# One more pair of row tiles by Strassen's scheme in the output product of a two-layer encoder, and earlier token sums

## The chip, the cores and the metric

The kernel runs on one core of one Trainium2 chip. Its time is device microseconds (us), the median of repeated runs. The core has a TensorE (in the profile PE for matmuls and PEld for weight loads), a VectorE (DVE), a ScalarE (ACT), a GpSimd (POOL), and queues that issue DMAs; nearly all DMAs here are issued by SyncE (SP).

## What is computed

Two layers, each on x of 256 tokens by 2048 columns in float32:

```python
for l in range(DEPTH):                       # DEPTH = 2
    h = rmsnorm(x, norm_g[l])
    proj = h @ w_in[l]                       # 2048 x 7168, split into ten groups
    y_a = conv3(a_c * a_x) * a_b * silu(a_g)     # 768 columns: 6 row tiles of y
    y_d = differential attention, 6 heads        # 768 columns: 6 row tiles
    y_m = attention into 256 memory tokens, 4 heads  # 512 columns: 4 row tiles
    y = concatenate([y_a, y_d, y_m]) @ w_out[l]  # 2048 x 2048
    x = x + y
```

The change lies in the last product, y @ w_out[l], and in how its operands are prepared.

## The kernel before

**Products.** Every float32 operand is split into a high and a low part in float32r (`hi`, a cast on ACT, and `lo`, the difference on DVE), and one product of a 128x128 token tile with a 128x512 weight tile is three matmuls: high by high, high by low, low by high (`products`, L305; `product`, L351). The activations are kept transposed, 16 row tiles k of 128 columns each, with 256 tokens: `yT` holds y. Tiles 0 to 5 are the conv group, 6 to 11 the differential heads, 12 to 15 the memory heads. Tile 6 + n is ready once head n is done; `made` records it.

**Pieces.** `block` goes through row tiles two at a time. One such weight piece is 256 rows by 512 columns of a weight matrix, 512 KB. `load_w` issues its DMA on SP into one of four `raw` buffers (L291), casts it on ACT (L294) and makes the low part on DVE (L295), into one of four `hi` and four `lo` buffers. A piece then feeds 12 matmuls: two row tiles, two token halves, three matmuls each. A `hi` or `lo` buffer is free again when the matmuls of the piece four before are done. After each piece `run_side` advances the tasks: generators that do the work beside the products (attention, gates, turns through DRAM) a few instructions at a time; `later(g, n)` makes a task due n pieces on.

**Order.** What is wrapped in `pin` (`keep_in_program_order`) keeps the program's order on its engine; the rest is placed by a list scheduler that works on a timeline at build time. DMAs of `carry` (turns through DRAM) and the wide loads below are pinned.

**The output product before.** PSUM has four accumulator banks (`acc`) and four more (two `s`, two `t`), which attention uses earlier. w_out's 2048 columns are four blocks b of 512. Blocks 0 and 1 are begun with the ten head tiles (five pieces each), then finished with the six conv tiles (three pieces each), because the conv group comes last. `leave` adds a finished block to the residual `xs` (L1230) and, in layer 0, starts the turn of that quarter for the next layer. Blocks 2 and 3 are then made together: some pairs of row tiles (two pairs in layer 0, three in layer 1, `places`) go by Strassen's scheme in Winograd's form over both column blocks (`seven`), the rest by `block`, block 2 first.

**`seven`.** For one pair of row tiles and 1024 columns it loads two 128x1024 weight tiles (`wide`, L373, 512 KB each), makes seven weight operands from them with four subtractions (L380), a half-size split `one` and three full splits (L377), and does seven products of three matmuls (L351) where the plain way has eight. Products land in the two accumulators of the near block, the two of the far block, and four banks x1, x5, x6, x7 in `s` and `t`. `collect` later adds those four to the residual: a copy on ACT (L1266) and eight additions on DVE (L1262). The token side needs four sums per pair, made by `token_sums` (L356 to L366) in the task `all_sums`: one `f` addition, four additions of 128 columns, a cast and a difference. They live in buffers that earlier work leaves free (`mkT0`, `mkT1`, `v`). The task is started after the C_C block, eight pieces before the output product begins.

In this text T0, T1 and so on are the weight pieces counted from the start of a layer's output product. With the heads of block 0 at T0 to T4 and of block 1 at T5 to T9, the conv pieces follow at T10 to T15.

Of the kernel before, what the change touches and what calls it, by code (L numbers as in the profile page):

```python
# [10 lines left out]
F32 = mybir.dt.float32  # L11
# [7 lines left out]
P = 128  # L19
# [13 lines left out]
NB = 512  # L33
# [15 lines left out]
def encoder(ctx: ExitStack, tc: tile.TileContext, x, mem, norm_g, w_in, conv_w, conv_b,  # L49
# [21 lines left out]
    def nm(s):  # L71
        uid[0] += 1
        return f"{s}_{uid[0]}"
# [140 lines left out]
    def later(g, n):  # L214
        due[id(g)] = chunk[0] + n
        return g
# [151 lines left out]
    def seven(stat, k, sums, w, col0, c_near, c_far, x, first, last, homes, meanwhile):  # L368


        a, b = (pl.tile([P, 2, NB], F32, tag=tag, name=nm("wide")) for pl, tag in homes)
        for j, raw in enumerate((a, b)):
            pin(nc.sync.dma_start(raw.rearrange("p j c -> p (j c)"), w[(k + j) * P:(k + j + 1) * P, col0:col0 + 2 * NB]))  # L373

        def split(src, to=None):
            hi, lo = to or parts_tiles()
            return ((hi, pin(nc.scalar.copy(hi, src))), (lo, pin(nc.vector.tensor_tensor(lo, src, hi.bitcast(F32), ALU.subtract))))  # L377

        def minus(dst, v, u):
            pin(nc.vector.tensor_tensor(dst, v, u, ALU.subtract))  # L380

        def side_of(parts, j):
            return [v[:, j] for v, _ in parts]

        one = keep.tile([P, 2, 1, NB], F32R, tag="mga", name=nm("one"))
        b11 = split(a[:, 0:1], (one[:, 0], one[:, 1]))
        minus(a[:, 0], a[:, 1], a[:, 0])
        minus(a[:, 1], b[:, 1], a[:, 1])
        b2 = split(b)
        minus(b[:, 1], b[:, 1], a[:, 0])  # L390
        minus(b[:, 0], b[:, 0], b[:, 1])
        meanwhile()
        t13 = split(a)
        t42 = split(b)

        def tokens(j, t):
            return [stat[:, part, k + j, t * P:(t + 1) * P] for part in range(2)]

        def summed(i):
            return [sums[:, part, i] for part in range(2)]  # L400

        x1, x5, x6, x7 = x
        product(tokens(0, 0), x1, side_of(b11, 0), first, last)
        product(tokens(1, 0), c_near[0], side_of(b2, 0), False, False)
        product(summed(3), c_far[0], side_of(b2, 1), first, False)
        product(summed(0), x5, side_of(t13, 0), first, last)
        product(summed(2), x7, side_of(t13, 1), first, last)
        product(tokens(1, 1), c_near[1], side_of(t42, 0), False, False)
        product(summed(1), x6, side_of(t42, 1), first, last)
# [54 lines left out]
    def sheet(home, tag, n=NB // P):  # L464
        return home.tile([P, NA, n, NT, B], F32, tag=tag, name=nm("sh"))
# [200 lines left out]
    def mem_scores(l, h, st):  # L666
        while l not in queries:
            yield 1
        qT, parts = queries[l]
        q, k, g = qT[:, h], mkT[l][:, h], mgain[:, l:l + 1]  # L670
        qh, ql, kh, kl = (parts[:, j] for j in (2 * (h % 2), 2 * (h % 2) + 1, 4, 5))
        pin(nc.scalar.copy(qh, q))
        pin(nc.vector.tensor_tensor(ql, q, qh.bitcast(F32), ALU.subtract))
        pin(nc.scalar.activation(kh, k, AF.Copy, scale=g))
        pin(nc.vector.scalar_tensor_tensor(kl, k, g, kh.bitcast(F32), ALU.mult, ALU.subtract))
        yield 1
        sc = P ** -0.5
        s = ps_s.tile([P, NT, SEQ], F32, tag="s", name=nm("s"))
        for i in range(NT):
            at = slice(i * P, (i + 1) * P)  # L680
            nc.tensor.matmul(s[:, i, :], qh[:, at], kh, start=True, stop=False)  # L681
            nc.tensor.matmul(s[:, i, :], qh[:, at], kl, start=False, stop=False)  # L682
            nc.tensor.matmul(s[:, i, :], ql[:, at], kh, start=False, stop=True)  # L683
        mx = small.tile([P, NT], F32, tag="mmx", name=nm("mmx"))
        nc.vector.tensor_reduce(mx, s, AX.X, ALU.max)
        nc.vector.tensor_scalar(mx, mx, -sc, None, ALU.mult)
        sm = small.tile([P, NT], F32, tag="msm", name=nm("msm"))
        e = tmp.tile([P, NT, SEQ], F32, tag="e", name=nm("me"))
        for i in range(NT):
            nc.scalar.activation(e[:, i], s[:, i], AF.Exp, bias=mx[:, i:i + 1], scale=sc, accum_out=sm[:, i:i + 1])  # L690
        r = small.tile([P, NT], F32, tag="mr", name=nm("mr"), bufs=6)
        nc.vector.reciprocal(r, sm)
        nc.vector.tensor_tensor(r, r, st[:, HR], ALU.mult)
        for i in range(NT):
            nc.vector.tensor_scalar(e[:, i], e[:, i], r[:, i:i + 1], None, ALU.mult)
        return e

    spare, yTs, gates, summed_heads = {}, {}, {}, set()

    def mem_pair(l, n, st):  # L700
        heads = (2 * n, 2 * n + 1)
# [361 lines left out]
    for l in range(DEPTH):  # L1063
# [9 lines left out]
        def x_block(cols, order=ALLK, **how):  # L1073
            return block(xT, w_in[l], cols, order, rows=x_row_tiles, **how)
# [101 lines left out]
        def both_rows(dst, j0, j1):  # L1176
            return [by_columns(dst[:, :, j0:j1, t]) for t in range(NT)]

        def scaled(dst, acc, by):
            for t in range(NT):  # L1180
                nc.scalar.activation(dst[t], columns(acc[t]), AF.Copy, scale=col(st, by, t))
# [10 lines left out]
        acc = x_block([(C_G, NB)])  # L1192
        gate(0, NB, acc)
        tasks.append(later(turn_bg(list(range(CG))), 9))
        acc = x_block([(C_X, NB)])
        ux = sheet(keep, "bgx", CG)
        scaled(both_rows(ux, 0, 4), acc, R2)
        acc = x_block([(C_C, NB)])
        times(both_rows(ux, 0, 4), acc)
        tasks.append(later(conv([0, 1, 2, 3], ux), 6))  # L1200
        sums = []

        def all_sums(l, yT, sums):
            for n, tag in enumerate(("mkT0", "v") if l + 1 < DEPTH else ("mkT0", "mkT1", "v")):
                while tag == "v" and (l, MH // 2 - 1) not in summed_heads:
                    yield 1
                sums.append(keep.tile([P, 2, 4, P], F32R, tag=tag, name=nm("sums")))
                yield from token_sums(yT, CG + 2 * n, sums[n])
                yield 1

        tasks.append(later(all_sums(l, yT, sums), 1))
        acc = x_block([(C_X + NB, 256), (C_C + NB, 256)])
        scaled(both_rows(ux, 4, 6), [a[:, 0:256] for a in acc], R2)
        times(both_rows(ux, 4, 6), [a[:, 256:512] for a in acc])
# [4 lines left out]
            xT = T_tile("xT")  # L1219
        heads, convs = list(range(CG, KT)), list(range(CG))  # L1220

        accs = [block(yT, w_out[l], [(b * NB, NB)], heads, more=True) for b in range(2)]
        final = l + 1 == DEPTH

        def finish(b, acc, keep_order=lambda i: i):
            for t in range(NT):
# [12 lines left out]
        def leave(b, acc, keep_order=lambda i: i, n=5):  # L1239
            finish(b, acc, keep_order)  # L1240
            if not final:
                tasks.append(later(x_next(xT, l + 1, b), n))

        for b in range(2):
            block(yT, w_out[l], [(b * NB, NB)], convs, acc=accs[b])
            if b == 0:
                leave(b, accs[b])
# [3 lines left out]
        homes = [((tmp, tag),) * 2 for tag in ("sh", "e", "sh")] if final else [((tmp, "sh"),) * 2, ((keep, "bgx"), (keep, "ga"))]  # L1251
        rest = [k for k in heads + convs if not CG <= k < CG + 2 * len(places)]
        near, far = accumulators(), accumulators()
        x = [pl.tile([P, NB], F32, tag=tag, name=nm("x")) for pl, tag in ((ps_s, "s"), (ps_s, "s"), (ps_t, "t"), (ps_t, "t"))]

        def collect(near):

            def at(t, b):
                return xs[:, t, b * NB:(b + 1) * NB]

            def plus(dst, v, u):
                pin(nc.vector.tensor_tensor(dst, v, u, ALU.add))  # L1262

            x1, x5, x6, x7 = x
            u, v = (tmp.tile([P, NB], F32, tag="nat", name=nm("u"), bufs=3) for _ in range(2))
            pin(nc.scalar.copy(u, x1))  # L1266
            plus(at(0, 2), u, at(0, 2))
            plus(u, u, x6)
            plus(v, u, x7)
            yield 1  # L1270
            plus(at(1, 2), v, at(1, 2))
            if not final:
                leave(2, near, n=3)
            plus(u, u, x5)
            plus(at(0, 3), u, at(0, 3))
            yield 1
            plus(v, v, x5)
            plus(at(1, 3), v, at(1, 3))
            if final:
                leave(2, near)  # L1280

        def pair_at(n):
            def run(near):
                seven(yT, paired[n], sums[n], w_out[l], 2 * NB, near, far, x, n == 0, n == len(paired) - 1,
                      homes[n], (lambda: leave(1, accs[1], pin, 4)) if n == 0 else lambda: None)
                if n == len(paired) - 1:
                    tasks.append(later(collect(near), 5))
                run_side(1)
            return run

# [35 lines left out]
```

## Time and profile before

| | us |
|---|---|
| median of 3 runs | 919.62 (919.55 to 919.75) |
| the profiled execution | 919.16 |
| its span in the trace | 917.4 |
| PE busy | 911.9 |
| DVE busy | 720.1 |
| ACT busy | 515.8 |

The span reaches from the first to the last instruction that the profiler recorded; 1.76 us of the profiled execution lie around it. In a line of the timeline the columns are the start, the duration, the engine, the source line, the operation, the tiles (output, then inputs), the shape and the count; a bracket names how long the engine had been idle and who ended it. A duration reaches to the end of the write, so that successive instructions of an engine overlap in it. A line of the stretches table gives, for each engine, busy time and number of instructions, then the granted TensorE clock, the DMA engines' busy share and GB/s. A line of the groups table gives count, busy time and mean duration in ns, then the idle time before.

### The profile page before, as it was taken

What the parts mean: (1) busy time and instruction counts of PE and PEld (TensorE: products, weight loads), DVE (VectorE), ACT (ScalarE), POOL (GpSimd) and SP (SyncE); (2) the same over time, 40 slices, a digit from 0 to 9 for tenths busy, and PEclk for the clock granted to TensorE, in tenths of its full rate; (3) what the DMA queues carried; (4) which work ended last, traced back from release to release, by engine and by line L of the source; (5) the groups of instructions that cost most, each with busy time, mean ns of one, the idle gap of its engine ahead of it and who ended that gap; (6) DMA issues with size and microseconds to landing.
All of it is one profiled execution on the core that took longest, in us unless ns stands there. A gap on an engine that the chain in (4) does not pass through costs nothing.

```text
span 917.4 us, 12407 instructions
## 1 busy us (share of the span) xinstructions
PE 911.9 (99%) x4161; PEld 757.3 (83%) x4161; DVE 720.1 (78%) x1293; ACT 515.8 (56%) x798; POOL 38.3 (4%) x68
## 2 busy tenths in 40 slices
PE   9999999999999999999999999999999999999998
PEld 6888888888888888888888888888888888888887
DVE  5579978857799697677789857878898787588786
ACT  5667645675555556445556544578555565546352
POOL 2435010000000000000000000000000000000000
PEclk9999999999999999999999999999999999999999
DMA  8899878886679998979777867986889998968842
GB/s 288 289 243 248 287 247 229 244 222 197 188 206 238 247 256 235 263 243 241 264 215 228 275 203 213 268 239 178 236 231 221 266 260 227 268 215 234 275 161 92
DMA packets 244560, 215.15 MB, mean 235 GB/s; under 512 B 131976, under 2 KB 171720, under 8 KB 244496
## 3 DMA queue, kind: packets, MB, share of 16 engines
q1 hardware_dynamic: 239520, 208.71, 79.3%
q0 software_dynamic: 3776, 4.59, 2.1%
q10 hardware_dynamic: 1200, 1.07, 0.3%
q8 instruction: 32, 0.52, 0.2%
q14 instruction: 32, 0.26, 0.1%
HBM read 193.30 MB, written 21.00 MB: 234 GB/s over the span
## 4 chain that ended last, share of the span: by engine, by line
PE 99%; DMA 0%; ACT 0%; SPq 0%; DVE 0%; issue 0%; ACTq 0%
PE acc L305 92%; PE x L351 2%; PE po L519 1%; PE acc L351 1%; PE s L627 1%; PE po L749 1%; PE s L626 1%; PE acc L933 1%; PE pt L763 0%; DMA raw<-in_w_mem_kv_dram 0%; PE s L683 0%; PE s L681 0%; PE s L682 0%; PE rest L305 0%; ACT hi L915 0%; SPq L833 0%
## 5 line engine op out<-in xcount | busy, mean ns | idle before, releaser
L305 PE MATMUL acc<-hi,xT 128*128 128x512 f32 x1792 | 558.4, 390 | 0.0
L294 ACT CAST hi<-raw 128x1024 fp32r<-128x1024 f32 x270 | 283.9, 1053 | 277.3 <-PE acc L305 200.0
L295 DVE TENSOR_TENSOR lo<-raw,hi 128x1024 fp32r<-128x1024 f32 x270 | 329.0, 1222 | 126.7 <-ACT hi L294 124.5
L305 PEld LDWEIGHTS acc<-hi,xT 128*128 128x128 f32 x1792 | 336.3, 188 | 69.0
L305 PE MATMUL acc<-lo,xT 128*128 128x512 f32 x896 | 349.2, 390 | 0.0
L305 PEld LDWEIGHTS acc<-lo,xT 128*128 128x128 f32 x896 | 168.2, 188 | 33.6
L305 PE MATMUL acc<-hi,yT 128*128 128x512 f32 (+1 forms) x432 | 134.1, 388 | 0.0
L305 PEld LDWEIGHTS acc<-hi,yT 128*128 128x128 f32 x432 | 81.0, 188 | 16.7
L305 PE MATMUL acc<-lo,yT 128*128 128x512 f32 x216 | 83.7, 388 | 0.0
L305 PE MATMUL acc<-hi,memT 128*128 128x512 f32 x248 | 78.0, 392 | 0.0
L305 PEld LDWEIGHTS acc<-hi,memT 128*128 128x128 f32 x248 | 46.2, 188 | 9.3
L916 DVE SCALAR_TENSOR_TENSOR lo<-raw,cva,hi 128x1024 fp32r<-128x1024 f32 (+1 forms) x34 | 41.0, 1218 | 15.4 <-ACT hi L915 15.1
L305 PE MATMUL acc<-lo,memT 128*128 128x512 f32 x124 | 48.0, 391 | 0.0
L305 PEld LDWEIGHTS acc<-lo,yT 128*128 128x128 f32 x216 | 40.6, 188 | 8.4
L915 ACT ACTIVATE hi<-raw,cva 128x1024 fp32r<-128x1024 f32 (+1 forms) x34 | 36.5, 1101 | 12.4 <-DMA raw<-in_w_mem_kv_dram 12.2
L305 PEld LDWEIGHTS acc<-lo,memT 128*128 128x128 f32 x124 | 23.3, 188 | 5.5 <-DVE lo L916 0.8
L377 ACT CAST hi<-wide 128x1024 fp32r<-128x1024 f32 x15 | 15.6, 1050 | 16.3 <-DVE wide L380 6.9
L637 ACT ACTIVATE e<-e,mx 128x256 f32<-128x256 f32 x48 | 23.8, 500 | 1.4 <-DVE mx L633 1.3
L780 POOL DMA_DIRECT2D xt<-in_x_dram x32 | 21.5, 678 | 19.7 <-DVE rsy L189 13.6
L377 DVE TENSOR_TENSOR lo<-wide,hi 128x1024 fp32r<-128x1024 f32 x15 | 18.1, 1220 | 3.5 <-ACT hi L377 3.3
L264 ACT ACTIVATE xT<-xf,gx 128x256 fp32r<-128x256 f32 x32 | 14.3, 503 | 5.7 <-DVE xf L786 5.0
L631 DVE SCALAR_TENSOR_TENSOR e<-dist,s 128x512 f32<-128x512 f32 x24 | 15.7, 680 | 2.2 <-PE s L627 1.7
(210 smaller groups left out, 765.8 us busy)
## 6 DMA issues: line engine op xcount, KB each, us to landing
raw<-in_w_in_dram SPq DMA_DIRECT2D x192, 512.0 KB, 4.6
raw<-in_w_out_dram SPq DMA_DIRECT2D x54, 512.0 KB, 4.8
raw<-in_w_in_dram SPq DMA_DIRECT2D x64, 256.0 KB, 4.3
raw<-in_w_mem_kv_dram SPq DMA_DIRECT2D x30, 512.0 KB, 6.4
d<-sh SPq DMA_DIRECT2D x88, 128.0 KB, 4.2
sh<-d SPq DMA_DIRECT2D x72, 128.0 KB, 4.1
wide<-in_w_out_dram SPq DMA_DIRECT2D x10, 512.0 KB, 7.0
xs<-in_x_dram SPq DMA_DIRECT2D x4, 512.0 KB, 6.3
```

Of the source, the lines that this page charges most:

```text
L264: both = (nc.scalar.activation(hi, src, AF.Copy, scale=gain), nc.vector.scalar_tensor_tensor(lo, src, gain, hi.bitcast(F32), ALU.mult, ALU ...
L294: nc.scalar.copy(hi, raw)
L295: nc.vector.tensor_tensor(lo_, raw, hi.bitcast(F32), ALU.subtract)
L305: i = nc.tensor.matmul(acc, left, right, start=start, stop=stop)
L351: nc.tensor.matmul(acc, left[a], right[b], start=first and i == 0, stop=last and i == 2)
L377: return ((hi, pin(nc.scalar.copy(hi, src))), (lo, pin(nc.vector.tensor_tensor(lo, src, hi.bitcast(F32), ALU.subtract))))
L519: nc.tensor.matmul(po[:, t, :], eT[:, i, t, k, :], v[:, k, h * P:(h + 1) * P], start=k == 0, stop=k == NT - 1)
L631: nc.vector.scalar_tensor_tensor(e[:, c], dist, -slopes[h], s[c], ALU.mult, ALU.add)
L637: nc.scalar.activation(e[:, c, i], e[:, c, i], AF.Exp, bias=mx[:, c, i:i + 1], accum_out=sm[:, c, i:i + 1])
L780: tc.keep_in_program_order(nc.gpsimd.dma_start(st[:, n], src[n * B:(n + 1) * B].rearrange("p (b r) -> b p r", b=NA)))
L915: both = (nc.scalar.activation(hi[:, j], raw[:, j], AF.Copy, scale=g), nc.vector.scalar_tensor_tensor(lo[:, j], raw[:, j], g, hi[:, j].bit ...
L916: nc.vector.scalar_tensor_tensor(lo[:, j], raw[:, j], g, hi[:, j].bitcast(F32), ALU.mult, ALU.subtract))
```

## The change

In both layers the pair of row tiles 6 and 7 (differential heads 0 and 1) goes through `seven` for the column blocks 0 and 1, too. Blocks 0 and 1 then take four head pieces each (tiles 8 to 15) in place of five, and the wide pair is put between the third and the fourth piece of block 0. Its seven products go to the two accumulators of block 0, the two of block 1 (both pairs of accumulators are now taken up front), and the banks `s` and `t`; `collect`, due four pieces later, adds the four banks to the residual. The wide tiles and the `one` operand use the temporary buffers `sh`, `sh` and `e`. `sums[0]` serves both wide pairs of tiles 6 and 7. The task `all_sums` is started after the C_G block, 16 pieces sooner; it now waits until the two heads' tiles are made, and, for the buffer of the layer's own memory keys, until all memory heads are scored. With the new count the pieces of the output product are T0, T1, T2, the wide pair, the last head piece of block 0 (here p3), four of block 1 (b0 to b3), then the conv pieces V0 to V5. The two-way shape of blocks 2 and 3 stays.

```diff
     def seven(stat, k, sums, w, col0, c_near, c_far, x, first, last, homes, meanwhile):
-        a, b = (pl.tile([P, 2, NB], F32, tag=tag, name=nm("wide")) for pl, tag in homes)
+        a, b = (pl.tile([P, 2, NB], F32, tag=tag, name=nm("wide")) for pl, tag in homes[:2])
...
-        one = keep.tile([P, 2, 1, NB], F32R, tag="mga", name=nm("one"))
+        one = homes[2][0].tile([P, 2, 1, NB], F32R, tag=homes[2][1], name=nm("one"))
...
+        mem_scored.add((l, h))
...
         acc = x_block([(C_G, NB)])
         gate(0, NB, acc)
         tasks.append(later(turn_bg(list(range(CG))), 9))
+        sums = []
+
+        def all_sums(l, yT, sums):
+            for n, tag in enumerate(("mkT0", "v") if l + 1 < DEPTH else ("mkT0", "mkT1", "v")):
+                while not all((id(yT), CG + 2 * n + i) in made for i in range(2)):
+                    yield 1
+                while tag == f"mkT{l}" and not all((l, h) in mem_scored for h in range(MH)):
+                    yield 1
+                while tag == "v" and (l, MH // 2 - 1) not in summed_heads:
+                    yield 1
+                sums.append(keep.tile([P, 2, 4, P], F32R, tag=tag, name=nm("sums")))
+                yield from token_sums(yT, CG + 2 * n, sums[n])
+                yield 1
+
+        tasks.append(later(all_sums(l, yT, sums), 1))
         acc = x_block([(C_X, NB)])
...
         tasks.append(later(conv([0, 1, 2, 3], ux), 6))
-        sums = []
-
-        def all_sums(l, yT, sums):
...
-        tasks.append(later(all_sums(l, yT, sums), 1))
...
-        accs = [block(yT, w_out[l], [(b * NB, NB)], heads, more=True) for b in range(2)]
         final = l + 1 == DEPTH
+        accs = [accumulators() for _ in range(2)]
...
+        def banks():
+            return [pl.tile([P, NB], F32, tag=tag, name=nm("x")) for pl, tag in ((ps_s, "s"), (ps_s, "s"), (ps_t, "t"), (ps_t, "t"))]
+
+        def collect(b, x, then=lambda: None):
...
+            x1, x5, x6, x7 = x
+            u, v = (tmp.tile([P, NB], F32, tag="nat", name=nm("u"), bufs=3) for _ in range(2))
+            pin(nc.scalar.copy(u, x1))
+            plus(at(0, b), u, at(0, b))
+            plus(u, u, x6)
+            plus(v, u, x7)
+            yield 1
+            plus(at(1, b), v, at(1, b))
+            if not final:
+                then()
+            plus(u, u, x5)
+            plus(at(0, b + 1), u, at(0, b + 1))
+            yield 1
+            plus(v, v, x5)
+            plus(at(1, b + 1), v, at(1, b + 1))
+            if final:
+                then()
+
+        x = banks()
+
+        def early_pair(near):
+            seven(yT, CG, sums[0], w_out[l], 0, near, accs[1], x, True, True,
+                  ((tmp, "sh"), (tmp, "sh"), (tmp, "e")), lambda: None)
+            tasks.append(later(collect(0, x), 4))
+            run_side(1)
+
+        for b in range(2):
+            block(yT, w_out[l], [(b * NB, NB)], heads[2:], more=True, acc=accs[b], opened=(b == 1, False),
+                  between={6: early_pair} if b == 0 else {})
         for b in range(2):
             block(yT, w_out[l], [(b * NB, NB)], convs, acc=accs[b])
...
-        x = [pl.tile([P, NB], F32, tag=tag, name=nm("x")) for pl, tag in ((ps_s, "s"), (ps_s, "s"), (ps_t, "t"), (ps_t, "t"))]
+        x = banks()
...
-                      homes[n], (lambda: leave(1, accs[1], pin, 4)) if n == 0 else lambda: None)
+                      (*homes[n], (keep, "mga")), (lambda: leave(1, accs[1], pin, 4)) if n == 0 else lambda: None)
                 if n == len(paired) - 1:
-                    tasks.append(later(collect(near), 5))
+                    tasks.append(later(collect(2, x, lambda: leave(2, near) if final else leave(2, near, n=3)), 5))
```

More of the change, by code (lines that the diff above doesn't have):

```diff
@@ L696, in mem_scores @@
         return e
-    spare, yTs, gates, summed_heads = {}, {}, {}, set()
+    spare, yTs, gates, summed_heads, mem_scored = {}, {}, {}, set(), set()
     def mem_pair(l, n, st):
@@ L1200, in encoder @@
         tasks.append(later(conv([0, 1, 2, 3], ux), 6))
-        sums = []
-        def all_sums(l, yT, sums):
[L1204 to L1209, printed above, removed]
-        tasks.append(later(all_sums(l, yT, sums), 1))
         acc = x_block([(C_X + NB, 256), (C_C + NB, 256)])
@@ L1242, in leave, with at, plus @@
                 tasks.append(later(x_next(xT, l + 1, b), n))
+        def banks():
+            return [pl.tile([P, NB], F32, tag=tag, name=nm("x")) for pl, tag in ((ps_s, "s"), (ps_s, "s"), (ps_t, "t"), (ps_t, "t"))]
+        def collect(b, x, then=lambda: None):
+            def at(t, b):
+                return xs[:, t, b * NB:(b + 1) * NB]
+            def plus(dst, v, u):
+                pin(nc.vector.tensor_tensor(dst, v, u, ALU.add))
+            x1, x5, x6, x7 = x
[24 more added lines that the diff above has]
+                  between={6: early_pair} if b == 0 else {})
         for b in range(2):
@@ L1253, in encoder @@
         near, far = accumulators(), accumulators()
-        x = [pl.tile([P, NB], F32, tag=tag, name=nm("x")) for pl, tag in ((ps_s, "s"), (ps_s, "s"), (ps_t, "t"), (ps_t, "t"))]
[L1256 to L1280, printed above, removed]
+        x = banks()
         def pair_at(n):
```

## The prediction

> **What bounds the kernel now.** First the page: busy time, granted clock and the chain that ended last.
>
> ```profile
> span 917.4 us, 12407 instructions
> ...
> PE 911.9 (99%) x4161; PEld 757.3 (83%) x4161; DVE 720.1 (78%) x1293; ACT 515.8 (56%) x798; POOL 38.3 (4%) x68
> ...
> PEclk9999999999999999999999999999999999999999
> ...
> PE 99%; DMA 0%; ACT 0%; SPq 0%; DVE 0%; issue 0%; ACTq 0%
> ```
>
> PE is busy for all but 5.5 us, the chain is PE alone, and the clock is full in every slice. A busy PE need not be a full one, so next comes the view of waits, for PE:
>
> ```profile
> PE warm L128 <- DVE zeros L123: 1.2, 1, 1.2
> PE acc L933 <- ACT hi L915: 0.8, 1, 0.8
> ```
>
> These are all its waits, 2.0 us, and both lines belong to the start (warm-up and the first memory matmuls). Nowhere in the output products does PE wait. What a matmul then costs is the step from one start to the next, not its 0.39 us. The timeline of PE, first and last of 13 successive starts in a Strassen pair and the piece behind it:
>
> ```profile
> 469.76 0.39 PE L351 MATMUL x<-lo,sums 128*128 128x512 f32 x1
> ...
> 472.48 0.39 PE L305 MATMUL acc<-lo,yT 128*128 128x512 f32 x1
> ```
>
> Twelve steps in 2.72 us: 0.2267 us for one, and 2.72 us for a weight piece of 12. So the kernel is a row of matmuls without holes. It can gain only by fewer of them, and loses as soon as a weight piece is split too late.
>
> How late is too late is the lead: the time from the end of a piece's split on DVE to the first matmul that needs its low part. For T0 in layer 0 (DVE's split, PE's first use), and what ACT waits for in this stage:
>
> ```profile
> 413.70 1.23 DVE L295 TENSOR_TENSOR lo<-raw,hi 128x1024 fp32r<-128x1024 f32 x1 [1.50 <-ACT hi L294]
> ...
> 418.01 1.06 ACT L294 CAST hi<-raw 128x1024 fp32r<-128x1024 f32 x1 [1.66 <-PE acc L305]
> ...
> 420.76 0.39 PE L305 MATMUL acc<-lo,yT 128*128 128x512 f32 x1
> ```
>
> The split ends at 414.93, the use is at 420.76: a lead of 5.83 us. ACT waits for PE, that is for a split buffer to come free, so the lead is at the most that four buffers allow. T0 starts one matmul before that use, at 420.5.
>
> **What goes.** Per layer, tiles 6 and 7 took 2 x 2 x 2 products for two column blocks, 24 matmuls; seven products are 21. Three matmuls less are 3 x 0.2267 = 0.68 us, in two layers 1.36 us. Since PE has no holes, this is on the path in full. It is also the most that can be gained: no wait inside the output products is there to be removed. The profiled execution, 919.16, would be 917.80; the median of the runs, 919.62, stands 0.46 above it, and from the median I get 918.26.
>
> The Trainium skill, "TensorE: Matmul & The Clock Gate", section "Back-to-back issue gap", gives about 131 ns for a matmul of 512 columns in a sustained stream. Six matmuls would then be worth an estimated 0.79 us. The trace disagrees with 226.7 ns, and the measurement decides.
>
> **What is added, on DVE.** Durations of the groups, by shape:
>
> ```profile
> L377 DVE TENSOR_TENSOR lo<-wide,hi 128x1024 fp32r<-128x1024 f32 x15 | 18.1, 1220 | 3.5 <-ACT hi L377 3.3
> ...
> L380 DVE TENSOR_TENSOR wide<-wide 128x512 f32<-128x512 f32 x10 | 6.9, 692 | 0.3
> ...
> L1262 DVE TENSOR_TENSOR xs<-u,xs 128x512 f32<-128x512 f32 x8 | 5.3, 679 | 0.0
> ...
> L377 DVE TENSOR_TENSOR one<-wide,one 128x512 fp32r<-128x512 f32 x5 | 3.4, 687 | 0.3 <-ACT one L377 0.3
> ```
>
> and what the same kinds take when DVE is saturated and they follow each other (timeline, layer 0):
>
> ```profile
> 495.76 1.26 DVE L1262 TENSOR_TENSOR u<-u,x 128x512 f32<-128x512 f32 x2
> ...
> 500.87 3.48 DVE L295 TENSOR_TENSOR lo<-raw,hi 128x1024 fp32r<-128x1024 f32 x3
> ```
>
> That is 0.63 for 512 columns and 1.16 for a split. The pair costs one half split, four subtractions and three splits: 5 x 0.63 + 3 x 1.16 = 6.63, in place of two plain splits, 2.32: 4.31 more. `collect` has eight additions: 5.04. Together 9.35 us per layer (by the full durations 4.68 + 5.43 = 10.1). All of it falls between T0 and the conv pieces. Has DVE that time? The stretches table, for the ten head pieces of layer 0 and then of layer 1:
>
> ```profile
> 420.40:436.00 15.60, 15.60 (x71) 12.91 (x70) 13.21 (x23) 10.60 (x16) 0.00 (x0) 1.00 0.90 236
> 436.00:447.70 11.70, 11.70 (x53) 9.71 (x52) 9.73 (x15) 5.86 (x9) 0.00 (x0) 1.00 0.72 250
> ...
> 828.50:844.00 15.50, 15.50 (x71) 12.81 (x70) 13.63 (x23) 10.10 (x15) 0.00 (x0) 1.00 0.90 242
> 844.00:855.80 11.80, 11.80 (x54) 9.77 (x53) 9.32 (x15) 5.75 (x9) 0.00 (x0) 1.00 0.68 233
> ```
>
> In layer 0 DVE is busy for 22.94 of 27.3 us, 4.36 idle; in layer 1 22.95, so 4.35 idle. The new work overruns the idle time by 9.35 - 4.36 = 4.99, and PE gets there 0.68 sooner: 5.67 us of the 5.83 us of lead are eaten. Not all of the idle time can be used either. The two waits for the evacuation of the block before stay:
>
> ```profile
> 420.56 0.42 DVE L1185 TENSOR_TENSOR sh<-acc,sh 128x256 f32<-128x256 f32 x1 [0.23 <-ACT sh L1181]
> 421.24 0.42 DVE L1185 TENSOR_TENSOR sh<-acc,sh 128x256 f32<-128x256 f32 x1 [0.25 <-ACT sh L1181]
> ```
>
> With these 0.48 the first conv pieces are short by 0.3 us in layer 0. By the full durations it is 1.1. I take 0.6, between the two and nearer to the saturated rows, since DVE will be saturated. So PE is to wait for about 0.6 us, around V0 and V1.
>
> ACT gets three casts and a half in place of two, and one copy of 512 columns: at most 2.5 times the 1.06 above, 2.7 us; in the same stretch of layer 0 it is idle for 27.3 - 16.46 = 10.8, which hides it. Behind the conv pieces DVE catches up: one split of 1.16 per 2.72 us.
>
> **What is moved, on the queues.** The wide loads are pinned on SP, behind T2's load and the first turn of the conv group. SP's own timeline, layer 0 and layer 1, and the landing time of `wide`:
>
> ```profile
> 410.73 2.79 SPq L498 DMA_DIRECT2D d<-sh  x4
> 413.62 1.73 SPq L291 DMA_DIRECT2D raw<-in_w_out_dram  x2
> 415.44 6.05 SPq L502 DMA_DIRECT2D uT<-d  x4
> ...
> 447.98 0.94 SPq L373 DMA_DIRECT2D wide<-in_w_out_dram  x2
> ...
> 817.89 1.95 SPq L498 DMA_DIRECT2D d<-sh  x4
> ...
> 823.25 4.73 SPq L502 DMA_DIRECT2D uT<-d  x4
> ```
>
> ```profile
> DMA to landing us min/median/max: 4.5/7.0/8.7
> ```
>
> They take 0.94 us to issue, from about 413.6, and land by 421.5 (8.7: 423.2). From the second tile's landing the last operand needs a cast, a split, two subtractions and two splits: 1.05 + 1.22 + 1.38 + 2.44 = 6.1 us, so it is there by 427.6 (429.3). The pair starts at 420.5 + 3 x 2.72 = 428.7, and the sixth product needs it 16 matmuls on, at 432.3: 3 us to spare. In layer 1 the loads go out at 819.84, 8.7 us before T0 at 828.5, against 6.9 in layer 0, so DVE can begin 1.8 us sooner there; that covers the 0.6, and I forecast no wait in layer 1. Bytes don't change (two of 512 KB for two of 512 KB); uT goes out 0.9 later and is not needed before V0.
>
> The banks `s` and `t` are free: the last attention result of layer 0 is read out in
>
> ```profile
> 400.20 0.41 DVE L752 TENSOR_TENSOR sh<-po,sh 128x256 f32<-128x256 f32 x1
> ```
>
> 28 us before the pair. The token sums for this pair are moved, not added; they stood here in layer 0:
>
> ```profile
> 394.80 0.68 DVE L356 TENSOR_TENSOR f<-yT 128x512 f32<-128x512 f32 x1
> ...
> 405.08 0.69 DVE L366 TENSOR_TENSOR sums<-sums,sums 128x512 fp32r<-128x512 f32 x1
> ```
>
> PE did not wait there, so nothing comes back. Where they go, the products of the C_X block cover them, as far as the lead there holds (a rival below, with its price); they issue no DMA, and I cost the move at nothing. Sum: 919.62 - 1.36 + 0.6 = 918.9.
>
> **The rivals.**
>
> *DVE falls further behind (slower).* The order on DVE is fixed at build time. If the last conv groups stand ahead of V0's split as well, that split waits for one of them more:
>
> ```profile
> L1167 DVE SCALAR_TENSOR_TENSOR z<-uT,cvb,z 128x255 f32<-128x255 f32 x12 | 5.7, 478 | 0.0
> ...
> L1170 DVE TENSOR_TENSOR z<-z,bgT 128x256 f32<-128x256 f32 x12 | 5.1, 424 | 0.3
> ```
>
> A group is two of the first kind and two like the second: 1.8 us. With full durations layer 0 is short by 1.1 + 1.8 = 2.9, layer 1 by 1.1 without its head start's help, and 1.8: together 5.8, so 924.1. It decides for slower from 1.36 + 1.84 = 3.2 us of waits in all. For it: the lead is used up to the last half microsecond. Against it: in the saturated stretch at 486 to 504 splits are let in between the additions, and PE kept on.
>
> *The wide loads come late.* If they stand behind uT, they go out at 421.5 and 828.0, land some 7.9 us later, and the last operand is there at 435.5 and 842.0 against needs of 432.3 and 840.3: waits of 3.2 and 1.7, in all 4.9, so 923.2. Against it: `wide` at 447.98 stands directly behind its piece's load, and uT is issued two pieces later in the program.
>
> *Half clock after such a wait.* At the start, behind an idle PE, the matmuls of the same shape are longer:
>
> ```profile
> L933 PE MATMUL acc<-hi,memT 128*128 128x512 f32 x8 | 3.6, 597 | 0.8 <-ACT hi L915 0.8
> ```
>
> Eight of 597 ns, not 390: 8 x 0.207 = 1.7 us more, 924.9 in all. It needs one wait as long as 3.2 us. The same page of the Trainium skill, section "What's actually happening", says that an idle window of about 3.4 us halves the clock; the start agrees in kind, and no later row here shows it.
>
> *The token sums meet a thin lead.* In the C_X block of layer 0, where they go, DVE is full and the lead small. A split on DVE, and PE's first use of its low part:
>
> ```profile
> 361.57 1.21 DVE L295 TENSOR_TENSOR lo<-raw,hi 128x1024 fp32r<-128x1024 f32 x1
> ```
>
> ```profile
> 364.09 0.40 PE L305 MATMUL acc<-lo,xT 128*128 128x512 f32 x1
> ```
>
> The lead is 364.09 - 362.78 = 1.31. The sums take 0.68 and 0.69 (above) and four additions of
>
> ```profile
> L361 DVE TENSOR_TENSOR sums<-f 128x128 f32<-128x128 f32 x5 | 1.4, 285 | 0.0
> ```
>
> 0.285: 2.5 us. All ahead of this split, PE waits 1.2 us: 920.1 with the 0.6 of the forecast. They are emitted over three pieces, which speaks against it.
>
> *The change does less than it says* (fewer matmuls saved) I rule out: the count follows from the loops.
>
> **How the numbers follow.** Forecast, 0 to 1.9 us of waits (918.3 to 920.2): 0.72. DVE further behind: 0.11. Wide loads late: 0.06, and half clock behind it 0.01. Sums on a thin lead: 0.08. Faster than the matmuls explain: 0.02. Range 918.1 to 921.0: it leaves out the slow rivals. A measurement of this kernel tells about 0.2% from no change, 1.84 us: same from 917.8 to 921.5. The slow rivals make 0.18, of which 0.02 stay under that bound: slower 0.16, faster 0.02, same 0.82.
>
> **What would show it.** PE instructions fall from 4161 to 4155. The step between matmuls stays at 0.227. DVE is at 10.0 of 10.0 us from about 422 to 455 in layer 0, and the lead at V0 and V1 is near zero; the view of waits gives PE a line or two of under a microsecond on L295. A wait at L351 on `hi`, `lo` or `one` of `wide` means late loads. Leads of 2 us and more at V0 and no wait would show the shortage wrong (918.3); waits over 3.2 us in all would make the forecast wrong in sign.

## The result and the profile after

The changed kernel takes 926.57 us (925.36 to 927.08, 5 runs) against 919.55 (918.00 to 919.75, 5 runs) beside it: a ratio of 1.0078 (in brackets, here and below, the 95% interval: [1.0064, 1.0093]). It is slower by 7.0 us, where the forecast was 918.9 and the range ended at 921.0. The profiled execution took 927.08.

The page of the kernel after, rows in the order of those shown of before:

```profile
span 925.3 us, 12428 instructions
...
PE 915.0 (99%) x4155; PEld 757.4 (82%) x4155; DVE 735.3 (79%) x1321; ACT 518.1 (56%) x804; POOL 38.2 (4%) x68
...
PEclk9999999999999999999989999999999999999999
...
PE 97%; DMA 2%; SPq 1%; DVE 0%; ACT 0%; issue 0%; ACTq 0%
```

Six matmuls are gone, as computed. But the granted TensorE clock is below full in slice 21 (463 to 486 us), and the chain of waits now holds DMA and SP. The view of waits, for PE, names them:

```profile
PE x L351 <- ACT one L377: 3.3, 1, 3.3
...
PE x L351 <- ACT hi L377: 0.8, 2, 0.5
PE acc L351 <- ACT hi L377: 0.4, 2, 0.2
...
PE acc L305 <- DVE xs L1235: 0.2, 1, 0.2
```

None is on L295, where the forecast had put its 0.6 us. All on L351 stand in the Strassen products of blocks 2 and 3, 20 us and more behind the place that the forecast watched. The chain of waits from 440 to 486 us, in order of time (start, us, what):

```profile
462.84 0.24 PE acc L305
...
463.11 1.30 DVE xs L1235 x2
...
464.42 2.77 DMA xd<-xs
...
467.21 0.33 SPq L771
...
469.07 6.22 DMA wide<-in_w_out_dram
...
475.31 0.63 ACT one L377
```

Read forwards: block 0 ends, `leave` adds it to the residual, SP writes that quarter of x out (`xd`), waits for it to land, issues its four turned loads (`xt`, L771), and only then may issue the wide loads of the second pair of blocks 2 and 3, which are pinned behind them on the same queue. PE needs `one`, the first operand from these loads, and stands still. What became late? The ends of blocks 0 and 1 (and the last conv tile), before and after, from DVE's timelines; before:

```profile
444.72 0.42 DVE L1172 TENSOR_TENSOR yT<-z,yT 128x256 fp32r<-128x256 f32 x1
...
455.60 1.28 DVE L1230 TENSOR_TENSOR xs<-acc,xs 128x512 f32<-128x512 f32 x2
...
463.57 1.37 DVE L1230 TENSOR_TENSOR xs<-acc,xs 128x512 f32<-128x512 f32 x2 [0.53 <-PE acc L305]
```

after:

```profile
460.03 0.42 DVE L1173 TENSOR_TENSOR yT<-z,yT 128x256 fp32r<-128x256 f32 x1
...
463.11 1.29 DVE L1235 TENSOR_TENSOR xs<-acc,xs 128x512 f32<-128x512 f32 x2 [0.20 <-PE acc L305]
...
465.63 1.28 DVE L1235 TENSOR_TENSOR xs<-acc,xs 128x512 f32<-128x512 f32 x2
```

The last conv tile is made 15.3 us later. A third of this lateness is there when the conv group starts, before `collect` adds anything. The group's first instruction is an activation on ACT; from ACT's timelines, before:

```profile
424.42 0.60 ACT L1166 ACTIVATE z<-uT,cvb 128x256 f32<-128x256 f32 x1
```

after:

```profile
425.69 1.05 ACT L377 CAST hi<-wide 128x1024 fp32r<-128x1024 f32 x1 [1.67 <-PE acc L305]
...
429.37 0.60 ACT L1167 ACTIVATE z<-uT,cvb 128x256 f32<-128x256 f32 x1
```

It starts 5.0 us later, behind the last of the pair's casts. Both are pinned, and that cast waits for PE. (The tasks also advance by one step for the pair's 21 matmuls; which of the two holds the group up was not tried alone.)

In the old order block 0's last piece would begin some 5.4 us behind V0, at about 452, and PE would have waited for that tile (worked out, not tried). It shows no such wait: block 0 ends 7.5 us later, block 1 only 2.1 us later, and 2.5 us lie between the two ends in place of 8.0. Block 1's three conv pieces take 36 steps, 8.2 us, so most of them now stand ahead of block 0's end: the list scheduler lays out PE's work too. PE loses nothing by this up to 463 us. What pays is the queue behind block 0. SP's timeline before and after:

```profile
456.92 0.37 SPq L804 DMA_DIRECT2D xd<-xs  x1
...
464.17 0.92 SPq L373 DMA_DIRECT2D wide<-in_w_out_dram  x2
```

```profile
464.42 0.37 SPq L805 DMA_DIRECT2D xd<-xs  x1
...
469.07 0.92 SPq L373 DMA_DIRECT2D wide<-in_w_out_dram  x2
```

And PE's timeline at the place:

```profile
472.28 0.39 PE L305 MATMUL acc<-hi,yT 128*128 128x512 f32 x1
475.98 0.79 PE L351 MATMUL x<-one,yT 128*128 128x512 f32 x1 [3.31 <-ACT one L377]
...
481.69 0.53 PE L305 MATMUL acc<-lo,yT 128*128 128x512 f32 x1
482.05 0.40 PE L305 MATMUL acc<-hi,yT 128*128 128x512 f32 x1
```

From 472.28 to the next start is 3.70, less a step of 0.2267: 3.47 us of wait. Then 14 steps take 6.07 us, at 0.427 most of them, where 14 x 0.2267 = 3.17 would do: 2.90 us for half clock (a stretch in which the granted clock is half). Shorter waits of the same stage (463 to 470), for the `leave` that stands ahead on DVE and for casts that stand behind the squares of the leaving quarters on ACT, add 1.62. In the last layer no quarter goes on to another layer, but there, too, block 0 ends late, and both blocks' stores are issued on ACT in one lump ahead of the pair's casts:

```profile
879.12 3.65 ACTq L1240 DMA_DIRECT2D out_dram<-xs  x4
882.81 1.99 ACT L377 CAST hi<-wide 128x1024 fp32r<-128x1024 f32 x2 [7.56 <-DVE xs L1235]
```

PE's waits there make 1.6 us.

### The profile page after: what moved, and what is told of

Its sections match the earlier page's. It is cut to its first block, busy times and chain, and to the rows that moved or that the text cites. A ratio compares the mean times of both kernels' runs of the same rounds, so it can differ in the third digit from the quotient of the medians.

```text
span 925.3 us, 12428 instructions
## 1 busy us (share of the span) xinstructions
PE 915.0 (99%) x4155; PEld 757.4 (82%) x4155; DVE 735.3 (79%) x1321; ACT 518.1 (56%) x804; POOL 38.2 (4%) x68
## 4 chain that ended last, share of the span: by engine, by line
PE 97%; DMA 2%; SPq 1%; DVE 0%; ACT 0%; issue 0%; ACTq 0%
PE acc L305 89%; PE x L351 2%; PE acc L351 1%; PE po L519 1%; DMA raw<-in_w_mem_kv_dram 1%; DMA wide<-in_w_out_dram 1%; PE s L627 1%; PE po L750 1%; PE s L626 1%; DMA xd<-xs 0%; PE pt L764 0%; DVE xs L1235 0%; PE s L683 0%; PE s L681 0%; PE s L682 0%; SPq L897 0%
## 5 line engine op out<-in xcount | busy, mean ns | idle before, releaser
L294 ACT CAST hi<-raw 128x1024 fp32r<-128x1024 f32 x266 | 279.1, 1051 | 274.7 <-PE acc L305 205.9
L295 DVE TENSOR_TENSOR lo<-raw,hi 128x1024 fp32r<-128x1024 f32 x266 | 323.7, 1221 | 114.4 <-ACT hi L294 112.9
L305 PE MATMUL acc<-hi,yT 128*128 128x512 f32 (+1 forms) x400 | 127.4, 393 | 0.3 <-DVE xs L1235 0.2
L305 PEld LDWEIGHTS acc<-hi,yT 128*128 128x128 f32 x400 | 76.2, 191 | 17.1 <-PE acc L305 0.6
L305 PE MATMUL acc<-lo,yT 128*128 128x512 f32 x200 | 78.3, 393 | 0.0
L305 PEld LDWEIGHTS acc<-lo,yT 128*128 128x128 f32 x200 | 38.3, 191 | 7.9
L377 ACT CAST hi<-wide 128x1024 fp32r<-128x1024 f32 x21 | 21.8, 1047 | 24.4 <-DVE wide L380 8.0
L377 DVE TENSOR_TENSOR lo<-wide,hi 128x1024 fp32r<-128x1024 f32 x21 | 25.5, 1221 | 5.3 <-ACT hi L377 5.2
```

The lines of the kernel that those rows point to most:

```text
L294: nc.scalar.copy(hi, raw)
L295: nc.vector.tensor_tensor(lo_, raw, hi.bitcast(F32), ALU.subtract)
L305: i = nc.tensor.matmul(acc, left, right, start=start, stop=stop)
```

## The account by stages

One matmul marks each cut in PE's timeline: the 1149th (in layer 0, well ahead of the change), the 3192nd of before (the 3189th where three are saved), and the last. This removes the beginning, where waits for the first loads differ by up to 2 us between executions.

| kernel | start of the first mark | layer 0's part | layer 1's part | span |
|---|---|---|---|---|
| before | 258.64 | 444.39 | 210.49 | 917.4 |
| after | 258.12 | 451.81 | 211.52 | 925.3 |
| e1 (no additions) | 257.88 | 444.41 | 210.07 | 916.2 |
| e2 (own queue) | 259.86 | 445.40 | 211.49 | 920.4 |
| e3 (additions later) | 259.00 | 448.01 | 210.39 | 921.3 |
| e4 (reordered) | 259.80 | 443.75 | 210.85 | 918.3 |
| e5 (sums as before) | 258.80 | 452.45 | 211.52 | 926.6 |
| e6 (8 additions) | 259.09 | 444.79 | 210.49 | 918.6 |
| e7 (15 additions) | 258.41 | 447.22 | 211.04 | 920.5 |
| e8 (reordered, stores moved) | 258.88 | 443.75 | 209.86 | 916.2 |

Layer 0 of the changed kernel is 7.42 us longer: 3.47 + 2.90 + 1.62 - 0.68 = 7.31, so 0.1 is not placed. Layer 1 is 1.03 longer: 1.6 - 0.68 = 0.9.

## The experiments

Three theories. **A**: the added VectorE work makes the conv tiles late, so block 0 ends late, and what is queued behind its end (the next layer's quarter and the wide loads on SP) goes out late. **B**: the wide loads of the third block are late for reasons of their own. **C**: the moved token sums hold up the conv work. Edits are against the changed kernel unless said. The first four were compared with 919.05 us (917.95 to 921.18, 26 runs) of the kernel before, the last four with 919.04 (917.97 to 919.93, 22 runs).

**e1_no_collect.** The early pair is kept, `collect`'s eight additions for it and the copy on ACT are left out; the output lacks the four products that they would have added.

```diff
+            def no_collect():
+                yield 1
...
-            tasks.append(later(collect(0, x), 4))
+            tasks.append(later(no_collect(), 4))
```

> Leaves out the early pair's collect: its four banks are never added to the residual, so columns 0 to 1023 lack those terms. Theory A (the added VectorE work makes the conv tiles late, block 0 of the output product ends late with them, and the next layer's quarter 0 and the wide loads behind it on SP are late in turn): with 5 us less on VectorE block 0 ends about 2 us behind its place and not 8, no wait of several us is left, 918.3 to 919.5. Theory B (the third block's wide loads are late for reasons of their own, buffers or queue, whatever the conv tiles do): unchanged, about 926. Theory C (the token sums, moved, hold up the conv work): unchanged, about 926.

Measured: 918.54 us, ratio 0.9993 [0.9983, 1.0003]. From DVE's timeline:

```profile
451.48 0.42 DVE L1173 TENSOR_TENSOR yT<-z,yT 128x256 fp32r<-128x256 f32 x1
456.73 1.29 DVE L1235 TENSOR_TENSOR xs<-acc,xs 128x512 f32<-128x512 f32 x2 [2.45 <-PE acc L305]
```

Block 0 ends 6.4 us sooner than in the changed kernel, and the loss is gone, while the token sums stay moved and the wide loads stay where they are in the program. B and C fall. The conv group still starts as late as in the changed kernel, and its last tile is 6.8 us later than before the change; this alone costs PE no more than the short waits named next. Layer 0's part is 444.41, not 443.71: the pair's own splits alone cost some 0.7 us here, in short waits for casts of the later pairs (`one` among them) and not for a weight split.

**e2_xnext_pool.** The next layer's first quarter goes through GpSimd's queue, so that the wide loads need not stand behind it.

```diff
-    def strips_of(src):
+    def strips_of(src, eng):
...
-            tc.keep_in_program_order(nc.sync.dma_start(
+            tc.keep_in_program_order(eng.dma_start(
...
-        st = strips_of(src) if l else strips_by_rows(src, after)
+        st = strips_of(src, nc.gpsimd if q == 0 else nc.sync) if l else strips_by_rows(src, after)
...
-        tc.keep_in_program_order(nc.sync.dma_start(d.rearrange("t p c -> p t c"), xs[:, :, q * NB:(q + 1) * NB]))
+        tc.keep_in_program_order((nc.gpsimd if q == 0 else nc.sync).dma_start(d.rearrange("t p c -> p t c"), xs[:, :, q * NB:(q + 1) * NB]))
```

> The turn of quarter 0 for the next layer is issued on POOL's queue, so that the wide loads of layer 0's second late pair don't stand behind it on SP. Theory A: the 3.5 us wait and the half-clock stretch behind it (about 3 us) go, the 1.6 us of short waits in each layer stay: 919.5 to 920.5. Theory B with the queue as the reason: the same. Theory B with the buffers as the reason, and theory C: about 926.

Measured: 920.72 us, ratio 1.0018 [1.0008, 1.0027], 0.2 above the expected band. SP's timeline:

```profile
454.01 2.77 SPq L373 DMA_DIRECT2D wide<-in_w_out_dram  x2
```

The wide loads go out 15 us sooner though block 0 ends as late as without the edit. The long wait and the half clock are gone: layer 0's part falls by 6.41, and the two were 3.47 + 2.90 = 6.37. The short waits stay in both layers (445.40 is 1.0 over before, 211.49 as in the changed kernel). The link from block 0's end over SP to PE is shown.

**e3_collect_late.** The additions become due seven pieces on, not four.

```diff
-            tasks.append(later(collect(0, x), 4))
+            tasks.append(later(collect(0, x), 7))
```

> The early pair's collect comes three pieces later, behind most of the conv work. Theory A, with collect alone as what makes the conv tiles late: about 918.3 to 919.5. Theory A, with the conv group held up by the pair's own casts and by the missing piece step as well: block 0 still ends with block 1, 922 to 926. Theories B and C: about 926.

Measured: 922.94 us, ratio 1.0037 [1.0024, 1.0051]: over half of the loss stays, as the second of A's bands has it (922 to 926) and not the first. The conv tiles are as late as in the changed kernel (the last one on DVE at 461.66), and the wide loads go out at 469.97. Here three pieces of postponement only move the additions to another spot among the conv work. PE's timeline has a surprise:

```profile
477.76 0.73 PE L351 MATMUL x<-one,yT 128*128 128x512 f32 x2 [0.16 <-DVE one L377]
479.11 0.50 PE L351 MATMUL acc<-hi,yT 128*128 128x512 f32 x1 [0.62 <-ACT hi L377]
479.45 0.39 PE L351 MATMUL acc<-hi,sums 128*128 128x512 f32 x1
480.37 1.05 PE L351 MATMUL x<-hi,sums 128*128 128x512 f32 x2 [0.53 <-ACT hi L377]
481.22 0.63 PE L351 MATMUL acc<-lo,yT 128*128 128x512 f32 x1
```

The starts from 480.37 are 0.427 apart: half clock, without one long wait. More of it below.

**e4_reordered.** The pair comes two pieces sooner, the conv tasks' first step is three pieces long, one turn of the tasks more is given for the pair's length (21 matmuls count as one piece of 12), and the additions become due ten pieces behind the pair, not four.

```diff
-        tasks.append(later(conv([0, 1, 2, 3], ux), 6))
+        tasks.append(later(conv([0, 1, 2, 3], ux, wait=3), 6))
...
-            tasks.append(later(collect(0, x), 4))
+            tasks.append(later(collect(0, x), 10))
+            run_side(1)
...
-                  between={6: early_pair} if b == 0 else {})
+                  between={2: early_pair} if b == 0 else {})
```

> The pair stands behind the first piece and takes two steps of the tasks, the conv group's turn comes two pieces sooner and collect later, so that the conv tiles are in time and block 0 again ends before block 1 begins its conv pieces. Theory A: no wait of PE over 0.5 us in the output products, 918.0 to 918.8, below the kernel before by the 1.36 us of the six matmuls. Theory B: 922 or more. Theory C: about 926, since the sums stay where the change put them.

Measured: 918.68 us, ratio 0.9997 [0.9988, 1.0007]. Layer 0's part is 443.75, 0.64 under before: there the three matmuls are all that is left. Layer 1 is 0.36 over before. ACT's timeline shows the likely reason (e8 tests it):

```profile
873.30 2.41 ACTq L1240 DMA_DIRECT2D out_dram<-xs  x2
875.80 2.00 ACT L377 CAST hi<-wide 128x1024 fp32r<-128x1024 f32 x2 [8.09 <-DMA out_dram<-xs]
```

Two stores take 2.41 us to issue ahead of the pair's casts; in the kernel before such a couple took 1.02. Why one issue now lasts 1.2 us stays open.

**e5_sums_old.** The task of the token sums is started where it was (its definition, left out here, moves with it).

```diff
-        tasks.append(later(all_sums(l, yT, sums), 1))
         acc = x_block([(C_X, NB)])
...
         tasks.append(later(conv([0, 1, 2, 3], ux), 6))
+        tasks.append(later(all_sums(l, yT, sums), 1))
```

> The changed kernel with the token sums made where they were made before, behind the C_C block; the early pair stays. A (the added VectorE work makes the last conv tiles late, block 0 ends late, and the next layer's first quarter and the third block's wide loads go out late on SP): as the changed kernel, 925 to 928. C (the moved token sums hold up the conv work): the loss goes with the move, 918.0 to 920. B (wide loads late for reasons of their own) tells nothing else than A here.

Measured: 928.12 us, ratio 1.0093 [1.0077, 1.0109], 0.1 above the expected band. Its interval overlaps that of the changed kernel. The move of the sums costs nothing and saves nothing that these runs can tell; C falls by a second way.

**e6_load8 and e7_load15**, both against the kernel before. No pair, no saved matmul, no moved sum or load: only idle additions on DVE, eight where `collect` has them, and for e7 seven more where the pair's splits stand; each group has two ACT copies ahead of it, to fill its operands. Their sums are used nowhere. In `busy`, e6 has the last line alone.

```diff
+        def spend():
+            u, v = (tmp.tile([P, NB], F32, tag="nat", name=nm("u"), bufs=3) for _ in range(2))
+            pin(nc.scalar.copy(u, xs[:, 0, 0:NB]))
+            pin(nc.scalar.copy(v, xs[:, 1, 0:NB]))
+            for n in (3, 3, 2):
+                for i in range(n):
+                    pin(nc.vector.tensor_tensor(v, u, v, ALU.add))
+                yield 1
+        def busy(near):
+            u, v = (tmp.tile([P, NB], F32, tag="nat", name=nm("u"), bufs=3) for _ in range(2))
+            pin(nc.scalar.copy(u, xs[:, 0, 0:NB]))
+            pin(nc.scalar.copy(v, xs[:, 1, 0:NB]))
+            for i in range(7):
+                pin(nc.vector.tensor_tensor(v, u, v, ALU.add))
+            tasks.append(later(spend(), 4))
-        accs = [block(yT, w_out[l], [(b * NB, NB)], heads, more=True) for b in range(2)]
+        accs = [block(yT, w_out[l], [(b * NB, NB)], heads, more=True, between={8: busy} if b == 0 else {}) for b in range(2)]
```

> The kernel before, with nothing moved and no pair added, plus the load of `collect` alone: per layer one ScalarE copy more than `collect` has and eight VectorE additions of 512 columns at the turns where the changed kernel has them; their sums are used nowhere. 5.0 us against 4.36 us idle on VectorE and a lead of 5.83. A: conv tiles still early enough, PE's order stays block by block: 919.0 to 920.0, no change. B and C: no change.

> As e6_load8, with seven more such additions three pieces further up, where the pair's own splits and subtractions stand: 15 x 0.63 = 9.45 us per layer, about the 9.35 us that the change adds; their sums are used nowhere. No matmul, no load and no token sum differs from the kernel before. A: the same loss without the change: PE takes the two conv blocks in turns, block 0 ends late, xd and the wide loads follow late on SP: 922 to 928, against 919.05. B and C: 919 to 920, since neither the wide loads nor the sums are touched. The forecast as recorded (shortage shows as late weight splits): about 919.6.

Measured: e6 919.59 us, ratio 1.0006 [0.9997, 1.0015], no change. e7 922.30 us, ratio 1.0039 [1.0026, 1.0053]. From e7's DVE, SP, PE:

```profile
455.79 0.42 DVE L1172 TENSOR_TENSOR yT<-z,yT 128x256 fp32r<-128x256 f32 x1
...
461.39 0.69 DVE L1247 TENSOR_TENSOR xs<-acc,xs 128x512 f32<-128x512 f32 x1 [0.17 <-PE acc L305]
```

```profile
468.02 0.92 SPq L373 DMA_DIRECT2D wide<-in_w_out_dram  x2
```

```profile
472.45 0.39 PE L305 MATMUL acc<-hi,yT 128*128 128x512 f32 x1
474.52 0.50 PE L351 MATMUL x<-one,yT 128*128 128x512 f32 x1 [1.68 <-ACT one L377]
474.86 0.39 PE L305 MATMUL acc<-lo,yT 128*128 128x512 f32 x1
```

The pattern comes back without the pair, from idle additions and their copies: the late tile (11.1 us later than before), the late block 0 (461.39 against 455.60), the late wide loads, the wait for `one`. Eight additions are borne, fifteen aren't. The loss is smaller than the changed kernel's: the conv group starts on time (424.50 on ACT), the tile is 4.2 us less late, the wait is 1.84 us (474.52 less 472.45, less a step), and no half clock follows it.

**e8_reordered_pool.** e4, with the stores that stood on ACT ahead of the casts moved to GpSimd's queue.

```diff
-                        eng = nc.scalar if lo else nc.sync
+                        eng = (nc.gpsimd if b < 2 else nc.scalar) if lo else nc.sync
```

> e4_reordered, and in the last layer the right halves of blocks 0 and 1 go out from GpSimd's queue and not from ScalarE's, where they stood 2.41 us ahead of the pair's casts and PE waited some 1.0 us. A: the last of the added waits goes and the six matmuls are all that is left: 919.05 - 1.36 = 917.7 (917.2 to 918.4), the first version below both kernels. If the issue on ScalarE was not what PE waited for: 918.5 to 919.0, as e4.

Measured: 917.75 us (11 runs), ratio 0.9985 [0.9976, 0.9994]. It is the fastest of all. PE's waits are those of the beginning again:

```profile
PE warm L128 <- DVE zeros L123: 1.2, 1, 1.2
PE acc L934 <- ACT hi L916: 0.8, 1, 0.8
```

Both layers are under before, by 0.64 and 0.63: together 1.27 of the 1.36 that six matmuls are worth. So the Strassen pair pays what was computed, once block 0 ends in time and no store stands ahead of the casts; the stores were what e4 still lost in layer 1 (210.85 there, 209.86 here). Part of e8's gain may be the moved stores alone; the kernel before with only these moved was not tried, but it has no wait there to lose.

## Why the prediction was wrong

**The gain was right.** Three matmuls a layer, 0.68 us; e8 shows 0.64 and 0.63.

**The shortage was there.** DVE was to be full from about 422 to 455 us and to fall some 5 us behind. The windows of the kernel after (us, PE, PEld, DVE, ACT, POOL, clock, DMA, GB/s):

```profile
422.00:455.00 33.00, 33.00 (x147) 27.28 (x147) 30.32 (x47) 18.77 (x25) 0.00 (x0) 1.00 0.83 246
435.40:447.10 11.70, 11.70 (x53) 9.68 (x53) 11.70 (x19) 6.36 (x9) 0.00 (x0) 1.00 0.79 258
```

From 435.40 on DVE is busy for 11.70 of 11.70 us, but over the whole stretch for 30.32 of 33.00: at its start two splits wait for their casts (0.78 and 0.87 us). How far DVE falls behind no view here measures; e6 and e7 bracket what it can bear, eight additions and not fifteen. The prediction's 0.63 and 1.16 us are each a little too long: they share out the last instruction's full duration, while the steps here are 0.60 (441.59 to 442.19) and 1.14 (443.18 to 444.32). By these steps the added work is 8.9 us, not 9.35, some 0.4 us less of a shortage.

**The step that failed** is "5.67 us of the 5.83 us of lead are eaten", with "PE is to wait for about 0.6 us, around V0 and V1" drawn from it. It charges the whole shortage to the weight splits. The splits kept leads of 2.7 us and more, and the conv tiles were late in their place, the last one by 15.3 us. The split behind the pair, and V0's (DVE's split and the first use on PE of each):

```profile
429.50 1.23 DVE L295 TENSOR_TENSOR lo<-raw,hi 128x1024 fp32r<-128x1024 f32 x1 [0.87 <-ACT hi L294]
...
440.12 1.21 DVE L295 TENSOR_TENSOR lo<-raw,hi 128x1024 fp32r<-128x1024 f32 x1
```

```profile
433.42 0.39 PE L305 MATMUL acc<-lo,yT 128*128 128x512 f32 x1
...
446.80 0.39 PE L305 MATMUL acc<-lo,yT 128*128 128x512 f32 x1
```

The first has a lead of 433.42 - 430.73 = 2.69, V0's 446.80 - 441.33 = 5.47. The prediction had named "leads of 2 us and more at V0" as the sign that the shortage is wrong (918.3). That inference was wrong, too: the shortage was there, and other work bore it. The weight splits of the plain pieces are not pinned, and here the list scheduler let them in among the pinned additions; what went back were the conv tiles. The rival "DVE falls further behind" had the right engine but the wrong victim (splits behind conv groups; it was conv groups behind splits). The casts on ACT were priced by their busy time, 2.7 us, and found hidden. That the pinned casts stand ahead of the conv group's first activation was not in the working: the group starts 5.0 us later behind them. In e1, with no addition, it starts as late (429.13) and its last tile is 6.8 us late.

**PE's order was taken as fixed.** The working followed the pieces T0 to V5 as the program has them. Late tiles did not stop PE; they changed what it did next, and with it the time at which block 0 ends. The kernel's description named the quarter of the next layer, but the working never followed block 0's end to SP. The row of SP quoted for the rival of late loads (`wide` at 447.98) was the first pair's of blocks 2 and 3; the second pair's, at 464.17, stood directly behind the quarter's `xt`, and whatever delays block 0 pushes it. e2 shows that it was this.

**The wide loads that the forecast watched were not late.** The early pair made PE wait in neither layer; those of the second pair of blocks 2 and 3 did, in layer 0.

**Half clock** had a chance of 0.01 and a price of 1.7 us. It came, in layer 0 alone, and cost 2.90: 14 slow steps, not eight. That it needs one wait as long as 3.2 us does not hold: e3 has it without one.

**The moved sums** cost nothing, as forecast (e5).

## What to carry to other kernels

When an engine off the critical path runs out of idle time, ask which of its products the build-time order will let slip, not only which one the bottleneck needs next; then follow the late one to every pinned queue behind it, to the end of the stage and beyond. A cheap test of such a budget is the load alone: idle instructions of the same length in the old kernel (e6, e7) show the wait before the change is written. And a saving of 1.4 us has no room for waits that touch the clock (2.90 us here).

## What the runs showed of the hardware

The half clock does not need one long wait. After 3.47 us of it, 14 steps were slow (6.07 us in all), and in e5, after 4.21 us, 13. In e3, between 477.21 and 480.37, five steps held 3.16 - 5 x 0.2267 = 2.03 us of waits in pieces of under 0.8, and eight slow steps followed, 1.8 us lost. In e7 a single wait of 1.84 us was followed by none, and in the changed kernel 1.26 us of short waits in the four steps from 467.84 to 470.01 by none. So it looks like a share of idle time in some stretch of about 3 us, not a single gap; five cases don't fix the threshold.

The stretches table has the granted clock itself, the third number from the end. The changed kernel, then e3:

```profile
471.71:475.13 3.42, 0.96 (x5) 0.46 (x3) 1.62 (x2) 0.00 (x0) 0.00 (x0) 1.00 0.92 240
475.13:478.54 3.41, 2.56 (x6) 2.08 (x7) 2.51 (x4) 1.99 (x3) 0.00 (x0) 0.50 1.05 404
```

```profile
480.59:484.00 3.41, 3.41 (x9) 2.25 (x9) 3.32 (x4) 2.12 (x3) 0.00 (x0) 0.50 0.73 128
```

It is half from 475.13 to 481.95 in the changed kernel and from 476.40 to 483.23 in e5, 6.8 us each, and for 3.41 us in e3. In the changed kernel it falls while PE still waits, 0.85 us ahead of the next matmul. The Trainium skill, "TensorE: Matmul & The Clock Gate", section "What's actually happening", says that the clock follows the activity in a free-running window of about 3.4 us. The traces agree in kind: the slow stretches are one and two times 3.41 us long, and the idle time in e3 is in pieces.
